# Where the spaced weight blocks lie against the streamed rows: one shift for 320 columns, one for 336

## The chip, the cores and the metric

The kernel runs on one core of a Trainium2 chip. The metric is the device time of one execution in microseconds (us), the median over several runs. TensorE (PE in the profile) multiplies: an instruction pair of a weight load (PEld) and a matmul, in which the loaded 128x128 weights stay and the columns of the other operand are streamed past them. ScalarE (ACT) and VectorE (DVE) prepare operands, GpSimd (POOL) does elementwise work beside them, and SyncE (SP) issues the transfers.

## The reference

One inference step of a hybrid decoder layer in float32, on 336 tokens (16 meta tokens, 256 of a prompt, 8 sequences of 8 new ones) of width 2048:

```python
h = rms_norm(x, norm_w)
proj = h @ w_in                       # 2048 x 20544
z, xbc, dt_raw, sc_b, sc_c, sc_h, sc_z, g_a, g_b = split_proj(proj)
# branch A: depthwise conv of width 4 on xbc, chunked state-space scan (SSD), gated group norm
y_a = y @ w_ssd_out                   # 4096 x 2048
# branch B: short conv of width 3
u_c = causal_dwconv(sc_c * sc_h, sconv_prev, sconv_w)
y_b = (sc_b * u_c * silu(sc_z)) @ w_sconv_out
merged = sigmoid(g_a) * y_a + sigmoid(g_b) * y_b
out = rms_norm(x + merged @ w_o, final_norm_w)
```

Beside it the new states of both convolutions and of the scan are returned.

## The kernel before, in words

Everything lies with channels on the 128 partitions and tokens along the row. A projection is cut into **units** of 128 output channels (`unit`, line 130). A unit takes the 2048 input channels in two halves; for each half `wblk` (line 96) brings one 128x1024 piece of weights (eight blocks of 128x128) and splits it in two: `hi`, rounded to the matmul's format by ACT (line 101), and `lo`, the rest, by DVE (line 102). The activations are kept split in the same way, in `hx` (halves `hhi` and `hlo`), for the first units in `uhi` and `ulo`, for the short convolution's output in `vhi` and `vlo`, for the scan's in `yh` and `yl`. A product is `hi*xh + hi*xl + lo*xh`, so a half has 3 x 8 = 24 matmuls (`mm`, line 125, all issued on line 127) and a unit 48, summed in one bank of the accumulator. Each matmul loads its own weights.

Three things say where the operands of a matmul lie and in which order they come.

The row of block `k` is `hhi[:, k, t0:T]`. Rows are 336 numbers (1344 bytes) apart, and `t0` is 0 (336 columns, for the scan's x and B), 12 (`TC`, 324 columns, for its C and for the inputs of the short convolution) or 16 (`META`, 320 columns, everything else). `vhi`, `vlo`, `yh` and `yl` have rows of 336 numbers too, of which 320 are used.

The weight blocks are **spaced** (`spaced`, line 93): a tile has room for 1280 numbers (`WB`), its blocks begin 144 numbers (`WS`, 576 bytes) apart, and the whole lies `16 * at` numbers, that is `at` times 64 bytes, behind the tile's start. `at` is given with each unit, from the names on line 91 or as `j % 4`.

The order of the 24 matmuls comes from `terms` (line 116) with one of three plans. RISE takes the eight rows upwards, first all `hi*xh`, then `hi*xl`, then `lo*xh`. TURNS takes `hi*xh` and `hi*xl` of a row one after the other. FALL2 takes the even rows downwards and then the odd ones, or the reverse, in steps of two.

The stages follow each other on PE in the order in which they are written. In the first (lines 183 to 340) the short convolution's inputs C and h (`conv_in`, lines 241 and 246), its gate z and its factor B (line 332) come for j = 0 to 15, the first of them on `uhi`. Then come 16 pairs of a gate unit g_b (line 448) and a unit of w_sconv_out on `vhi` (v, line 451). The third stage runs over eight groups of the scan: `weave` (line 789) interleaves units of the z (line 513), of the next group's B, C and x (`conv_tile`, line 471), of the output projection of the group before (`out_units`, line 747, four rows a product, 12 matmuls, on `yh`) and of the gate g_a (line 763) with the steps of the scan, which have their own small matmuls. Last come the remaining output and gate units and the projection w_o (line 853).

Nothing has costs or due times: the order on each engine is the order of the program. Weight tiles have three buffers each, so a transfer, a split and the matmuls of three successive halves overlap.

Of the kernel before, what the change touches and what calls it, by code (L numbers as in the profile page):

```python
# [9 lines left out]
AF = mybir.ActivationFunctionType  # L10
# [6 lines left out]
META = 16  # L17
TC = 12
TV = T - META
# [21 lines left out]
def fb(ap):  # L41
    return ap.bitcast(F32)
# [7 lines left out]
def tile_hybrid_step(ctx, tc, xT, w0, w1, w2, wdt, wso, wsc, wo, cmask, vec, hvec, convst, sconvst, xe_, fwe, h0T,  # L50
                     yA, yB, yE, convo, ssmp, ssms, sconvo):
    nc = tc.nc
    mult, add, sub = ALU.mult, ALU.add, ALU.subtract
# [33 lines left out]
    def col(base, i):  # L87
        return V[:, base + i:base + i + 1]

    latest = {}  # L90
    AT_S, AT_B, AT_G, AT_V, AT_Z, AT_H, AT_Y, AT_O = 3, 0, 1, 1, 2, 3, 1, 0

    def spaced(name, at):
        return wp.tile([P, WB], F32R, name=name)[:, 16 * at:16 * at + 8 * WS].rearrange("p (k m) -> p k m", m=WS)[:, :, :P]
# [16 lines left out]
                    tc.add_manual_dep(ins, a.name, mybir.DependencyInfo(mybir.DependencyClass.NoSync,  # L111
                                                                         mybir.DependencyReason.DATA), reason="step")

    RISE, TURNS, FALL2 = range(3)

    def terms(plan, hi, lo, xh, xl, nk):
        if plan == TURNS:
            return [(hi, x, k) for k in range(nk) for x in (xh, xl)] + [(lo, xh, k) for k in range(nk)]
        if plan == FALL2:
            even, odd = (list(range(i, nk, 2))[::-1] for i in range(2))  # L120
            return [(w, x, k) for w, x, q in ((hi, xh, even), (hi, xl, even), (hi, xl, odd), (hi, xh, odd), (lo, xh, odd),
                                              (lo, xh, even)) for k in q]
        return [(w, x, k) for w, x in ((hi, xh), (hi, xl), (lo, xh)) for k in range(nk)]

    def mm(out, hi, lo, xh, xl, base, nk, k0, first, last, plan=RISE):
        for i, (w, x, k) in enumerate(terms(plan, hi, lo, xh, xl, nk)):
# [3 lines left out]
    def unit(src, xh, xl, n, plan=RISE, at=0):  # L130
        pt = ps.tile([P, 512], F32, name="pj")
        for half in range(2):
            hi, lo = wblk(src[:, half * 1024:half * 1024 + 1024], at)
            mm(pt[:, :n], hi, lo, xh, xl, 0, 8, half * 8, half == 0, half == 1, plan)
        return pt[:, :n]

    def proj(src, t0, plan=RISE, at=0):
        return unit(src, lambda k: hhi[:, k, t0:T], lambda k: hlo[:, k, t0:T], T - t0, plan, at)
# [25 lines left out]
    def eights(ap, w=8):  # L164
        return ap.rearrange("p (b t) -> p b t", t=w)
# [17 lines left out]
    with tc.tile_pool(name="pa", bufs=2) as pa:  # L183
# [33 lines left out]
        for k in range(KT):  # L217
            split = nc.scalar.activation(uhi[:, k, :], ya[:, k, :], AF.Copy, scale=yan[:, k:k + 1])
            rest = nc.vector.scalar_tensor_tensor(ulo[:, k, :], ya[:, k, :], yan[:, k:k + 1], fb(uhi[:, k, :]), mult, sub)
            if k % 2 == 0:  # L220
                hi = wp.tile([P, WB], F32R, name="whi")
                lo = wp.tile([P, WB], F32R, name="wlo")
# [15 lines left out]
        def conv_in(j, pr, pre=None, fac=None, between=None):  # L238
            c_s = pa.tile([P, T - TC], F32, name="c_s")
            if fac is None:  # L240
                nc.scalar.activation(c_s, pre[0] if pre else pr(w2[16 + j], TC, FALL2, j % 4), AF.Copy)
            else:
                nc.vector.tensor_tensor(c_s, pr(w2[16 + j], TC, FALL2, j % 4), fac, mult)
            if between:
                between()
            ph = pre[1] if pre else pr(w2[32 + j], TC, TURNS, j % 4)
            up = pa.tile([P, 338], F32, name=f"up{j}" if j < 2 else "up", bufs=1 if j < 2 else 2)
            ups = eights(up[:, 258:338], 10)
            nc.vector.tensor_tensor(up[:, :258], c_s[:, 2:260], ph[:, 2:260], mult)  # L249
            nc.vector.tensor_tensor(ups[:, :, 2:10], eights(c_s[:, 260:]), eights(ph[:, 260:]), mult)  # L250
            return up, ups
# [71 lines left out]
        vhi = pa.tile([P, KT, T], F32R, name="vhi", bufs=1)[:, :, :TV]  # L323
        vlo = pa.tile([P, KT, T], F32R, name="vlo", bufs=1)[:, :, :TV]
        for j in range(KT):
            u = ((up0, ups0), (up1, ups1), u2)[j] if j < 3 else conv_in(j, proj)
            if j == 3:
                nc.sync.dma_start(HV, hvec)
                consts(C_SEG, C_ALL)
            if j < 2:  # L330
                continue
            rest = [(j, *u, lambda: proj(w2[48 + j], META, at=AT_S), lambda: proj(w2[j], META, at=AT_B))]
            if 4 < j < 7:
                o = j - 5
                rest.append((o, *((up0, ups0), (up1, ups1))[o], lambda: zf[o], lambda: bf[o]))
            for q, *a in rest:
                th = conv_out(q, *a)
                nc.scalar.activation(vhi[:, q, :], th, AF.Copy)
                nc.vector.tensor_tensor(vlo[:, q, :], th, fb(vhi[:, q, :]), sub)
# [105 lines left out]

        tab = tables(pa)
        for m in range(KT):
            pg = proj(w2[80 + m], META, at=AT_G)
            th = pa.tile([P, TV], F32, name="thg", tag="thz")
            nc.scalar.activation(th, pg, AF.Tanh, scale=0.5)  # L450
            py = unit(wsc[m], lambda k: vhi[:, k, :], lambda k: vlo[:, k, :], TV, at=AT_V)
            nc.vector.scalar_tensor_tensor(th, th, 1.0, py, add, mult)
            nc.sync.dma_start(mb_d[m], th)
            next(tab, None)
# [6 lines left out]
    with tc.tile_pool(name="pb", bufs=2) as pb:  # L461
# [7 lines left out]
        czs = CZ.rearrange("p (s i w) -> p s i w", s=2, w=40)  # L469

        def conv_tile(src, j, t0, out, cs):
            pp = proj(src, t0, TURNS if t0 else FALL2, j % 4)
            pad = pads[npad[0] % 2]
            npad[0] += 1
            smp = pad[:, 275:363].rearrange("p (b t) -> p b t", t=11)
            nc.scalar.activation(pad[:, 3 + t0:275], pp[:, :272 - t0], AF.Copy)  # L476
            nc.scalar.activation(smp[:, :, 3:11], pp[:, 272 - t0:].rearrange("p (b t) -> p b t", t=8), AF.Copy)
            nc.gpsimd.tensor_copy(smp[:, :, 0:3], cs[:, 1:9, :])  # L478
            nc.gpsimd.tensor_copy(cs[:, 0, :], pad[:, 272:275])  # L479
            nc.gpsimd.tensor_copy(cs[:, 1:9, :], smp[:, :, 8:11])  # L480
            i0 = META if t0 else 0
            acc = pb.tile([P, 360], F32, name="cacc")
            nc.scalar.activation(acc[:, i0:], pad[:, i0:360], AF.Identity, bias=col(V_CB, j), scale=col(V_CW, 4 * j))
            for k in range(1, 4):
                nc.vector.scalar_tensor_tensor(acc[:, i0:], pad[:, i0 + k:360 + k], col(V_CW, 4 * j + k),  # L485
                                               acc[:, i0:], mult, add)
            th = pb.tile([P, 360], F32, name="cth", bufs=1)
            nc.scalar.activation(th[:, i0:], acc[:, i0:], AF.Tanh)  # L488
            nc.vector.scalar_tensor_tensor(out[:, i0:272], th[:, i0:272], 1.0, acc[:, i0:272], add, mult)
            nc.vector.scalar_tensor_tensor(  # L490
                out[:, 272:].rearrange("p (b t) -> p b t", t=8),
                th[:, 272:360].rearrange("p (b t) -> p b t", t=11)[:, :, 3:11], 1.0,
                acc[:, 272:360].rearrange("p (b t) -> p b t", t=11)[:, :, 3:11], add, mult)
# [16 lines left out]
        def z_units(g, st):  # L510
            st["zs"] = []
            for t in range(4):
                pz = proj(w1[4 * g + t], META, at=AT_Z)
                z = pb.tile([P, TV + 4], F32, name="zs", bufs=4)
                th = pb.tile([P, 360], F32, name="cth", bufs=1)[:, :TV]
                nc.scalar.activation(th, pz, AF.Tanh, scale=0.5)
                nc.scalar.activation(z[:, :TV], pz, AF.Copy)
                nc.vector.scalar_tensor_tensor(z[:, :TV], th, 1.0, z[:, :TV], add, mult)
                st["zs"].append(z)
                yield  # L520
# [239 lines left out]

        def gate_units(m0, m1):
            for m in range(m0, m1):
                pg = proj(w2[64 + m], META, at=AT_H)
                if m < KT // 2:
                    th = pb.tile([P, 360], F32, name="cacc")[:, :TV]
                else:
                    th = pb.tile([P, TV + 4], F32, name="zs", bufs=4)[:, :TV]
                nc.scalar.activation(th, pg, AF.Tanh, scale=0.5)
                if m < KT // 2:
                    nc.sync.dma_start(sg_d[m], th)  # L770
                else:
                    old = pb.tile([P, 360], F32, name="cacc")[:, :TV]
                    nc.sync.dma_start(old, sg_d[m - KT // 2])
                    pair = [(q, t, fetch(q)) for q, t in ((m, th), (m - KT // 2, old))]
                    with tc.issue_after(latest["dve"]):
                        for q in pair:
                            merge(*q)
                yield
# [40 lines left out]
    with tc.tile_pool(name="pc", bufs=3) as pc_:  # L819
# [42 lines left out]
        for m in range(KE, KT):  # L862
# [3 lines left out]
            for half in range(2):  # L866
# [6 lines left out]
                for wide in ((True, False), (False, True))[half]:  # L873
                    for k in range(8):
                        w, x = (h, hx[:, :, 8 * half + k, :NA]) if wide else (l, hhi[:, 8 * half + k, :NA])
# [44 lines left out]
        fac = pc_.tile([P, NA], F32, name="fac", bufs=1)  # L920
# [129 lines left out]
```

## Time and profile before

| | |
|---|---|
| runs shown | 1812.24, 1812.73, 1813.86 us; median 1812.73 |
| the profiled execution | 1811.64 us, its span 1809.8 us |
| PE busy | 1802.9 us, 13006 matmul records |
| DVE, ACT, POOL busy | 1145.9, 830.4, 389.1 us |
| matmuls of line 127 | 11280 (7536 of 320 columns, 1824 of 324, 1920 of 336) |
| granted TensorE clock | 1.0 |

A matmul's busy time is the length of one instruction from its start to its modelled end, and successive ones overlap. How fast PE goes is read from the distance between starts in the order of time, not from that length.

### The profile page before, as it was taken

How to read it: one execution, taken by the hardware profiler on the slowest of the kernel's cores; microseconds unless marked ns; L12 is line 12 of the kernel's file. 1: busy time of each engine (PE TensorE's matmuls, PEld its weight loads, DVE VectorE, ACT ScalarE, POOL GpSimd, SP SyncE). 2: the span in 40 equal slices, each digit the busy share in tenths (PEclk: the TensorE clock that was granted, in tenths of full speed). 3: DMA queues.
4: the chain of work that ended last, by engine and by line, in shares of the span. 5: the costliest groups of instructions: out<-in, count | busy, mean ns of one | idle time of the engine just before them, and what ended most of it. 6: DMA issues, size and time to landing. Idle time of an engine off the chain costs nothing.

```text
span 1809.8 us, 32410 instructions
## 1 busy us (share of the span) xinstructions
PE 1802.9 (100%) x13006; PEld 1786.8 (99%) x13006; DVE 1145.9 (63%) x1696; ACT 830.4 (46%) x1269; POOL 389.1 (21%) x398
## 2 busy tenths in 40 slices
PE   9999999999999999999999999999999999999998
PEld 9999999999999999999999999999999999999998
DVE  7845544444543335668587777877878778776644
ACT  6433333333333334645656354564546546343543
POOL 0100000000000001153252433524334243400012
PEclk9999999999999999999999999999999999999999
DMA  7444444444544557457466574665746657476553
GB/s 257 146 152 148 151 151 148 149 152 154 155 158 163 164 164 233 147 180 248 151 205 226 176 244 152 209 216 180 244 153 216 205 169 253 154 244 213 185 178 130
DMA packets 117286, 331.33 MB, mean 183 GB/s; under 512 B 20944, under 2 KB 37904, under 8 KB 117136
## 3 DMA queue, kind: packets, MB, share of 16 engines
q1 hardware_dynamic: 116272, 327.89, 55.9%
q8 instruction: 102, 1.67, 0.4%
q10 hardware_dynamic: 864, 1.38, 0.2%
q14 instruction: 48, 0.39, 0.1%
HBM read 296.34 MB, written 32.88 MB: 182 GB/s over the span
## 4 chain that ended last, share of the span: by engine, by line
PE 99%; issue 0%; DVE 0%; POOLq 0%; POOL 0%; DVEq 0%
PE pj L127 92%; PE yb L664 2%; PE ms L650 1%; PE pj L232 1%; PE yb L599 1%; PE ms L548 1%; PE pj L876 1%; PE ms L232 0%; PE yb L727 0%; PE yb L902 0%; PE ms L551 0%; PE ms L201 0%; PE ms L550 0%; PE pj L352 0%; PE pj L351 0%; PE ms L712 0%
## 5 line engine op out<-in xcount | busy, mean ns | idle before, releaser
L127 PE MATMUL pj<-hx,whi 128*128 128x320 f32 (+2 forms) x5760 | 913.5, 310 | 0.0
L127 PEld LDWEIGHTS pj<-hx,whi 128*128 128x128 f32 x5760 | 863.9, 188 | 4.6 <-ACT pad L476 1.7
L102 DVE TENSOR_TENSOR wlo<-wraw,whi 128x1024 fp32r<-128x1024 f32 x470 | 595.3, 1267 | 403.9 <-PE pj L127 203.7
L101 ACT ACTIVATE whi<-wraw 128x1024 fp32r<-128x1024 f32 x470 | 497.2, 1058 | 751.7 <-PE pj L127 622.8
L127 PE MATMUL pj<-hx,wlo 128*128 128x320 f32 (+2 forms) x2880 | 483.2, 310 | 0.0
L127 PEld LDWEIGHTS pj<-hx,wlo 128*128 128x128 f32 x2880 | 439.6, 188 | 0.0
L610 POOL TENSOR_TENSOR h<-h,decS 128x512 f32<-128x512 f32 x64 | 76.4, 1228 | 147.5 <-PE ms L650 147.5
L255 POOL COPY SCS<-up 128x2 f32<-128x2 f32 x16 | 20.9, 1308 | 355.7 <-DVE up L249 325.5
L127 PE MATMUL pj<-yh,whi 128*128 128x320 f32 x512 | 96.7, 310 | 0.0
L127 PE MATMUL pj<-yl,whi 128*128 128x320 f32 x512 | 95.5, 308 | 0.0
L127 PE MATMUL pj<-yh,wlo 128*128 128x320 f32 x512 | 95.5, 308 | 0.0
L758 DVE TENSOR_TENSOR yan<-yan,pj 128x320 f32<-128x320 f32 x112 | 54.3, 485 | 63.0 <-PE pj L127 61.8
L485 DVE SCALAR_TENSOR_TENSOR cacc<-pad,V,cacc 128x360 f32<-128x360 f32 (+1 forms) x144 | 89.7, 623 | 2.0
L127 PEld LDWEIGHTS pj<-yh,whi 128*128 128x128 f32 x512 | 80.3, 188 | 2.0 <-issue 0.2
L478 POOL COPY pad<-cs 128x24 f32<-128x24 f32 x48 | 53.3, 1111 | 127.6 <-DVE cacc L485 115.9
L127 PEld LDWEIGHTS pj<-yl,whi 128*128 128x128 f32 x512 | 80.1, 187 | 0.0
L127 PEld LDWEIGHTS pj<-yh,wlo 128*128 128x128 f32 x512 | 80.1, 187 | 0.0
L479 POOL COPY cs<-pad 128x3 f32<-128x3 f32 x48 | 45.0, 938 | 80.6 <-ACT pad L476 80.1
L858 POOL TENSOR_TENSOR sacc<-sacc,sqf 128x320 f32<-128x320 f32 x13 | 15.4, 1181 | 191.5 <-ACT sqf L856 191.5
L582 POOL TENSOR_TENSOR xe<-xdt,tet 128x512 f32<-128x512 f32 (+1 forms) x24 | 30.3, 1264 | 105.6 <-DVE xdt L553 91.5
L488 ACT ACTIVATE cth<-cacc 128x360 f32<-128x360 f32 (+1 forms) x48 | 23.9, 498 | 39.9 <-DVE cacc L485 39.4
L127 PE MATMUL pj<-vhi,whi 128*128 128x320 f32 x256 | 42.0, 306 | 0.0
(284 smaller groups left out, 1646.0 us busy)
## 6 DMA issues: line engine op xcount, KB each, us to landing
wraw<-w SPq DMA_DIRECT2D x346, 512.0 KB, 3.8
wraw<-wso SPq DMA_DIRECT2D x64, 512.0 KB, 3.5
wraw<-wsc SPq DMA_DIRECT2D x32, 512.0 KB, 3.8
h<-h0T SPq DMA_DIRECT2D x32, 512.0 KB, 5.1
ssms<-h SPq DMA_DIRECT2D x32, 512.0 KB, 4.2
wraw<-wo SPq DMA_DIRECT2D x32, 512.0 KB, 3.8
xq_d<-xe SPq DMA_DIRECT2D x16, 320.0 KB, 3.4
W<-ac_d SPq DMA_DIRECT2D x8, 576.0 KB, 5.7
```

Of the source, the lines that this page charges most:

```text
L101: latest["act"] = nc.scalar.activation(hi, raw, AF.Copy).ins
L102: latest["dve"] = nc.vector.tensor_tensor(lo, raw, fb(hi), sub).ins
L127: latest["pe"] = nc.tensor.matmul(out, w[:, base + k], x(k0 + k), start=first and i == 0, stop=last and i == 3 * nk - 1).ins
L255: nc.gpsimd.tensor_copy(SCS[:, j, 0, :], up[:, 256:258])
L478: nc.gpsimd.tensor_copy(smp[:, :, 0:3], cs[:, 1:9, :])
L479: nc.gpsimd.tensor_copy(cs[:, 0, :], pad[:, 272:275])
L485: nc.vector.scalar_tensor_tensor(acc[:, i0:], pad[:, i0 + k:360 + k], col(V_CW, 4 * j + k), acc[:, i0:], mult, add)
L488: nc.scalar.activation(th[:, i0:], acc[:, i0:], AF.Tanh)
L582: nc.gpsimd.tensor_tensor(split(xe[c][:n]), split(xdt[c][:n]), bc(hv(tet[:n, c, :], g), [n, 8, HP]), mult)
L610: nc.gpsimd.tensor_tensor(split(h0[b]), split(h0[b]), bc(hv(decS[:, b, :], g), [P, 8, HP]), mult)
L664: nc.tensor.matmul(yb[q * HP:(q + 1) * HP, t, t0:t0 + n], x[:, h * HP:(h + 1) * HP], w[:, h, :], start=i == 0, stop=i == 3)
L758: nc.vector.tensor_tensor(ya[:, m, :TV], ya[:, m, :TV], pp[:, :TV], add)
```

## The change

The names of `at` become AT_V = 1, AT_Y = 3, AT_O = 3, AT_X = 1, AT_C = 2, AT_SC = 0; what has no name left takes `at` = 0. The plan TURNS is dropped. A plan LAST is added, which takes the rows upwards but begins with the last of the eight: 7, 0, 1, ... 6. The v units use it. `conv_tile` takes FALL2 for 324 columns as well as for 336. The h input of the short convolution goes from TURNS to RISE at the same `at` as before. With rows and blocks both 1 modulo 4 in units of 64 bytes, each unit's next weight block then begins, modulo 4, 1 unit past the row that is streamed where there are 320 columns (on `hx`, `vhi` and `yh`), and 0 units past it where there are 336. No instruction, transfer or wait is added or taken away.

```diff
-    AT_S, AT_B, AT_G, AT_V, AT_Z, AT_H, AT_Y, AT_O = 3, 0, 1, 1, 2, 3, 1, 0
+    AT_V, AT_Y, AT_O, AT_X, AT_C, AT_SC = 1, 3, 3, 1, 2, 0
...
-    RISE, TURNS, FALL2 = range(3)
+    RISE, LAST, FALL2 = range(3)
 
     def terms(plan, hi, lo, xh, xl, nk):
-        if plan == TURNS:
-            return [(hi, x, k) for k in range(nk) for x in (xh, xl)] + [(lo, xh, k) for k in range(nk)]
...
-        return [(w, x, k) for w, x in ((hi, xh), (hi, xl), (lo, xh)) for k in range(nk)]
+        return [(w, x, (k - (plan == LAST)) % nk) for w, x in ((hi, xh), (hi, xl), (lo, xh)) for k in range(nk)]
...
-                nc.scalar.activation(c_s, pre[0] if pre else pr(w2[16 + j], TC, FALL2, j % 4), AF.Copy)
+                nc.scalar.activation(c_s, pre[0] if pre else pr(w2[16 + j], TC, FALL2, AT_SC), AF.Copy)
...
-            ph = pre[1] if pre else pr(w2[32 + j], TC, TURNS, j % 4)
+            ph = pre[1] if pre else pr(w2[32 + j], TC, at=j % 4)
...
-            rest = [(j, *u, lambda: proj(w2[48 + j], META, at=AT_S), lambda: proj(w2[j], META, at=AT_B))]
+            rest = [(j, *u, lambda: proj(w2[48 + j], META), lambda: proj(w2[j], META))]
...
-            pg = proj(w2[80 + m], META, at=AT_G)
+            pg = proj(w2[80 + m], META)
...
-            py = unit(wsc[m], lambda k: vhi[:, k, :], lambda k: vlo[:, k, :], TV, at=AT_V)
+            py = unit(wsc[m], lambda k: vhi[:, k, :], lambda k: vlo[:, k, :], TV, LAST, AT_V)
...
-            pp = proj(src, t0, TURNS if t0 else FALL2, j % 4)
+            pp = proj(src, t0, FALL2, AT_C if t0 else AT_X)
...
-                pz = proj(w1[4 * g + t], META, at=AT_Z)
+                pz = proj(w1[4 * g + t], META)
...
-                pg = proj(w2[64 + m], META, at=AT_H)
+                pg = proj(w2[64 + m], META)
```

More of the change, by code (lines that the diff above doesn't have):

```diff
@@ L240, in conv_in @@
             if fac is None:
-                nc.scalar.activation(c_s, pre[0] if pre else pr(w2[16 + j], TC, FALL2, j % 4), AF.Copy)
+                nc.scalar.activation(c_s, pre[0] if pre else pr(w2[16 + j], TC, FALL2, AT_SC), AF.Copy)
             else:
-                nc.vector.tensor_tensor(c_s, pr(w2[16 + j], TC, FALL2, j % 4), fac, mult)
+                nc.vector.tensor_tensor(c_s, pr(w2[16 + j], TC, FALL2, AT_SC), fac, mult)
             if between:
                 between()
-            ph = pre[1] if pre else pr(w2[32 + j], TC, TURNS, j % 4)
+            ph = pre[1] if pre else pr(w2[32 + j], TC, at=j % 4)
             up = pa.tile([P, 338], F32, name=f"up{j}" if j < 2 else "up", bufs=1 if j < 2 else 2)
```

## The prediction

> **What bounds the kernel now.** I read the page's first lines, then the chain of waits, then the waits by engine, and last the order of time on TensorE.
>
> ```profile
> span 1809.8 us, 32410 instructions
> PE 1802.9 (100%) x13006; PEld 1786.8 (99%) x13006; DVE 1145.9 (63%) x1696; ACT 830.4 (46%) x1269; POOL 389.1 (21%) x398
> PEclk9999999999999999999999999999999999999999
> PE 99%; issue 0%; DVE 0%; POOLq 0%; POOL 0%; DVEq 0%
> L127 PE MATMUL pj<-hx,whi 128*128 128x320 f32 (+2 forms) x5760 | 913.5, 310 | 0.0
> L101 ACT ACTIVATE whi<-wraw 128x1024 fp32r<-128x1024 f32 x470 | 497.2, 1058 | 751.7 <-PE pj L127 622.8
> ```
>
> PE is busy for the whole span at the full granted clock, and 99% of the chain of waits is PE. The matmuls of L127 wait for nothing (idle before 0.0), and ACT, which splits the weights, waits 622.8 us for PE to give a weight buffer back. So the time is the number of matmuls times the distance from one start to the next. The 310 ns of a row is the length of one matmul, which overlaps its neighbours. The distance has to be read from the starts, in the order of time. In the fence below the columns are start, length of the merged piece, engine, line, operation and count. A unit of the projection is 48 matmuls (two halves of 24), so the start of a unit less that of the unit before, over 48, is the distance.
>
> ```profile
> 91.99 2.53 PE L127 MATMUL pj<-hx,whi 128*128 128x324 f32 x16
> 99.09 2.55 PE L127 MATMUL pj<-hx,whi 128*128 128x324 f32 x16
> 106.25 2.52 PE L127 MATMUL pj<-hx,whi 128*128 128x320 f32 x16
> 113.30 2.48 PE L127 MATMUL pj<-hx,whi 128*128 128x320 f32 x16
> 120.26 2.51 PE L127 MATMUL pj<-hx,whi 128*128 128x324 f32 x16
> 127.29 2.52 PE L127 MATMUL pj<-hx,whi 128*128 128x324 f32 x16
> ...
> 176.52 2.50 PE L127 MATMUL pj<-hx,whi 128*128 128x324 f32 x16
> 183.56 2.52 PE L127 MATMUL pj<-hx,whi 128*128 128x324 f32 x16
> 190.66 2.51 PE L127 MATMUL pj<-hx,whi 128*128 128x320 f32 x16
> 197.71 2.44 PE L127 MATMUL pj<-hx,whi 128*128 128x320 f32 x16
> 204.52 0.75 PE L127 MATMUL pj<-hx,whi 128*128 128x324 f32 x4
> ...
> 624.86 1.33 PE L127 MATMUL pj<-vhi,whi 128*128 128x320 f32 x8
> 626.02 1.30 PE L127 MATMUL pj<-vlo,whi 128*128 128x320 f32 x8
> 631.69 2.48 PE L127 MATMUL pj<-hx,whi 128*128 128x320 f32 x16
> 638.61 0.60 PE L127 MATMUL pj<-vhi,whi 128*128 128x320 f32 x3
> ```
>
> The reader is to see that the same instruction, 128x320, has several distances. Call **shift** the 64-byte unit in which the next weights begin, less the unit in which the row streamed now begins, modulo 4. The blocks of a spaced tile lie 9 units apart and the rows 21 (336 numbers), both 1 modulo 4; META (16 numbers) is 1 unit, TC (12) three quarters. The program of the kernel before puts the spaced tiles 1 unit past a multiple of 4, hx, yh and yl at 0, vhi, vlo and uhi at 2. So in rising order a unit with META has shift `at`+1, a wo unit `at`+2, an output unit (yh) `at`+2, a v unit `at`. The order FALL2 takes rows in steps of two: with all 336 columns its shift is `at`-1, with 324 it is `at`-1.75. Now the rows:
>
> - Shift 0, the z of the short convolution (S: 106.25 to 113.30, 7.05 us): 146.9 ns.
> - Shift 1, its B (113.30 to 120.26, 6.96 us): 145.0; but B from 197.71 to 204.52, 6.81 us: 141.9. So shift 1 has two steady patterns.
> - Shift 2, the gate g_b (G: 631.69 to 638.61, 6.92 us): 144.2.
> - Shift 1, v (624.86 to 631.69, 6.83 us): 142.3, made of 145.0 in its first 8 matmuls (to 626.02) and 5.67 us over 40 = 141.75 after them.
>
> **The change part by part.** It neither adds nor removes an instruction, a DMA or a wait. It writes the two halves of a weight tile at another offset (ACT 1058 ns, a DVE twin; same form, hidden under PE as the 622.8 us show) and reorders matmuls inside a unit. All that it can move is the distance. The other units touched:
>
> ```profile
> 701.15 2.62 PE L127 MATMUL pj<-hx,whi 128*128 128x336 f32 x16
> 708.52 2.57 PE L127 MATMUL pj<-hx,whi 128*128 128x336 f32 x16
> 715.74 2.61 PE L127 MATMUL pj<-hx,whi 128*128 128x336 f32 x16
> 723.01 2.65 PE L127 MATMUL pj<-hx,whi 128*128 128x336 f32 x16
> 730.48 0.75 PE L127 MATMUL pj<-hx,whi 128*128 128x320 f32 x4
> 737.52 2.51 PE L127 MATMUL pj<-hx,whi 128*128 128x320 f32 x16
> 741.04 0.45 PE L127 MATMUL pj<-hx,whi 128*128 128x320 f32 x2
> 1002.19 0.74 PE L127 MATMUL pj<-yh,whi 128*128 128x320 f32 x4
> 1003.95 0.45 PE L127 MATMUL pj<-yh,whi 128*128 128x320 f32 x2
> 1609.90 0.73 PE L127 MATMUL pj<-yh,whi 128*128 128x320 f32 x4
> 1611.60 0.59 PE L127 MATMUL pj<-yh,whi 128*128 128x320 f32 x3
> 1702.14 2.47 PE L127 MATMUL pj<-hx,whi 128*128 128x320 f32 x16
> 1709.05 0.45 PE L127 MATMUL pj<-hx,whi 128*128 128x320 f32 x2
> ```
>
> *320 columns, all to shift 1.* What distance will they have? The low end is 141.75 (v's steady part), the high end 145.0 (the first B). I take **142.4**: about four fifths of the matmuls in the first pattern and one fifth in the second, because v and one of the two B rows settle in the first, and since the units will mostly follow one another at the same shift, a pattern once reached has fewer occasions to be left. Matmuls are units times 48, 24 a weight tile for wso.
>
> - S, 14 units, 672: 146.9 to 142.4 is 4.5 ns, 3.0 us.
> - z of the SSD (Z, shift 3; 737.52 to 741.04 is 3.52 us over 24, 146.7), 32 units, 1536: 4.3 ns, 6.6 us.
> - g_a (H, shift 0 as S), 16 units, 768: 4.5 ns, 3.5 us.
> - output units in the weave (Y, shift 3; 1002.19 to 1003.95, 1.76 us over 12, 146.7), 56 tiles, 1344: 5.8 us.
> - G, 768: 144.2 to 142.4, 1.4 us. The wo units (O, shift 2; 1702.14 to 1709.05, 6.91 us, 144.0), 14 units, 672: 1.1 us.
> - B, 672, from the mean of its two rows, 143.5: 0.7 us.
> - v (768) and the last output units (1609.90 to 1611.60, 1.70 us over 12: 141.7; 192) stand at or under 142.4 already: together 0.2 us lost. Starting v from its last row makes the shift 1 at the borders from and to G too (in rising order they would be 2 and 0); it is worth at most the 8 x 3.25 ns of v's entry a unit, 16 units, 0.4 us, and lies in the 142.4.
>
> Sum 21.9 us over 7392 matmuls. Were all at 141.75 it would be 4.8 more, at 145.0 it would be 19.2 less.
>
> *336 columns, all to shift 0.* The four x units of the first group (701.15 to 730.48) have shifts 3, 0, 1, 2 and take 7.37, 7.22, 7.27 and 7.47 us: 153.5, 150.4, 151.5, 155.6. At the second's value they save 3.1, 0, 1.1 and 5.2 ns on 384 matmuls each: 3.6 us. The B units (8, 384 matmuls) run through the same four shifts twice: mean 152.75, 2.35 ns, 0.9 us. Ends: 150.4 is the lowest row; at the mean they would save nothing.
>
> *324 columns.* The first projection of the short convolution stands at `at` 3 (91.99 to 99.09, 147.9), 0 (120.26 to 127.29, 146.5) and 2 (176.52 to 183.56, 146.7); all go to 0: mean 147.0 to 146.5 on 624, 0.3 us. The C units of the SSD leave TURNS, which the h projection shows at 149.2 (99.09 to 106.25) and 147.9 (183.56 to 190.66), for FALL2 at the 146.7 of `at` 2: 1.9 ns on 384, 0.7 us. The h projection itself goes from TURNS to RISE at the same offsets; a whole unit of it in RISE is in no row. Its bounds are the highest and lowest 324 rows, 149.2 and 146.5 against a mean of 148.6: 0.4 us worse to 1.3 better on 624. I take 0.2 better, because a third of TURNS is in rising order already.
>
> All together 21.9 + 3.6 + 0.9 + 0.3 + 0.7 + 0.2 = **27.6 us**. The profiled execution took 1811.64 us (span 1809.8 and 1.84 around it), so 1784.0; the median of the runs shown is 1.09 higher, so **1785.1**.
>
> **What hides the rest.** If PE runs 1.5% faster, the splits must come 1.5% faster: per half a unit 1058 on ACT and, on DVE, the row below, against 3.42 us of matmuls (24 x 142.4). DVE's fullest slices are 8 tenths.
>
> ```profile
> DVE   7845544444543335668587777877878778776644
> L102 DVE TENSOR_TENSOR wlo<-wraw,whi 128x1024 fp32r<-128x1024 f32 x470 | 595.3, 1267 | 403.9 <-PE pj L127 203.7
> ```
>
> DVE too waits 203.7 us for PE at this line, so the cover holds. If it were gone in the eight groups of the SSD, their part of the sum (Z, Y, x, B, C and the gates in it, about 19 us) would be in question.
>
> The Trainium skill (TensorE: Matmul & The Clock Gate, "Step-by-step: what each phase is for") says that PE reads the streamed operand and the weights through two independent ports, so that loading the next weights takes no read bandwidth from the running matmul. By that rule the shift is worth nothing and the sum is 0. The rows of S and B, 146.9 against 141.9 for one form, speak against it.
>
> **The rivals.**
>
> 1. *The other pattern of shift 1.* 145.0 is as steady as 141.75. If after each break by the SSD's own matmuls, and after each 324 unit, the matmuls fall into it, the 320 columns gain 2.7 us instead of 21.9. For it: the first B. Against it: v. Time 1785.1 + 19.2 = 1804.3; with half of them so, 1794.7.
> 2. *Supply takes the place.* DVE becomes late in the groups and half of the 19 us goes: 1794.6. Against it: the 203.7 us.
> 3. *No effect.* The distance follows the neighbours in the stream and the place in the kernel, and the shift only goes along with them: each S comes after a 324 unit, each v after a G. Each unit keeps its distance: 1812.7. For it: shift 3 shows 146.7 in Y and 141.7 in the last output units. Against it: the x units, which differ in shift alone and run from 150.4 to 155.6.
> 4. *Slower.* The pattern is a lock between successive matmuls, kept from unit to unit; today the change of shift breaks bad ones, and with one shift everywhere the worst is kept: each width runs at its highest row. Then v loses 4.6 ns, G 2.7, O 2.9, B 3.4, the last output units 5.2 (3.5 + 2.1 + 1.9 + 2.3 + 1.0 = 10.8 us), and x and B units 155.6 less 152.75 on 1920, 5.5 us: 1829. The 320 columns average 145.4 now (142.4 plus 21.9 us / 7392); with the 5.7 us of the other units, 0.8 ns, it decides for slower from 146.2 on. Against it: v leaves 145.0 by itself within 8 matmuls and stays out:
>
> ```profile
> L127 PE MATMUL pj<-vlo,whi x256: 304/304/306, 465.9 to 685.4; 128*128 128x320 f32 x128
> ```
>
> All 256 matmuls of v's second pass have one length, in all 16 units.
>
> **How the numbers follow.** Forecast 0.76 (its own range 1779 to 1793: all 320 columns at 141.75 is 1780.3, four tenths more of them at 145.0 is 1793), rival 1 0.13 (1793 to 1805), rival 2 0.03, rival 3 0.04, rival 4 0.04. The range 1778 to 1800 holds the forecast, rival 2 and about half of rival 1. A measurement of this kernel can tell about 0.2%, 3.6 us, from no change: faster 0.92 (forecast, 1, 2), the same 0.04, slower 0.04.
>
> **What would show it.** Right: S, Z, H, Y, G and O units in the order of time at 6.80 to 6.85 us (1.70 for 12 matmuls of Y) with pieces 141.7 apart, x units all at 7.22, an unchanged number of instructions, PE still at 99% of the chain. Rival 1: B-like units of 6.96. Rival 2: a PE wait for `wlo` L102 that isn't there now. Wrong: S or Z units still at 7.05, or x units that still differ among themselves; then the shift isn't what sets the distance.

## The result, and the profile after

| | runs shown | median us | ratio to before, 95% interval |
|---|---|---|---|
| before | 4 (1812.24 to 1813.86) | 1812.95 | |
| changed | 4 (1786.97 to 1791.06) | 1789.39 | 0.9869 [0.9852, 0.9886] |

The change makes the kernel 23.6 us faster; 27.6 were forecast. The profiled execution of the changed kernel took 1786.97 us, which is its fastest run, 24.7 us below the profiled one of before. All lines after the dropped plan have moved up by two: line 127 is now 125, 621 is 619.

First the page of the changed kernel: span, engines, chain of waits and two groups.

```profile
span 1785.2 us, 32410 instructions
PE 1776.8 (100%) x13006; PEld 1760.2 (99%) x13006; DVE 1147.4 (64%) x1696; ACT 829.1 (46%) x1269; POOL 392.7 (22%) x398
PE 90%; DVE 4%; DMA 3%; ACT 2%; issue 1%; POOLq 0%; SPq 0%; POOL 0%; ACTq 0%; DVEq 0%
L102 DVE TENSOR_TENSOR wlo<-wraw,whi 128x1024 fp32r<-128x1024 f32 x470 | 599.5, 1276 | 389.2 <-PE pj L125 193.2
L125 PE MATMUL pj<-yh,whi 128*128 128x320 f32 x512 | 95.0, 307 | 1.5 <-ACT zs L515 0.8
```

The instructions are the same in number, and ACT and DVE have the same work to do. What is new is the third line: PE is 90% of the chain of waits, not 99%, and DMA, DVE and ACT have come into it. The last line shows where: the output units wait 0.8 us for ACT, which reads the scan's z out of the accumulator (`zs`, line 515); before, no matmul of that line did.

The units themselves, from the order of time on PE (start, length, engine, line, operation, count), in the places that the prediction quoted of before:

```profile
105.67 2.48 PE L125 MATMUL pj<-hx,whi 128*128 128x320 f32 x16
...
112.63 2.48 PE L125 MATMUL pj<-hx,whi 128*128 128x320 f32 x16
...
119.59 2.55 PE L125 MATMUL pj<-hx,whi 128*128 128x324 f32 x16
...
613.99 2.43 PE L125 MATMUL pj<-hx,whi 128*128 128x320 f32 x16
620.78 1.29 PE L125 MATMUL pj<-vhi,whi 128*128 128x320 f32 x8
627.59 2.43 PE L125 MATMUL pj<-hx,whi 128*128 128x320 f32 x16
...
696.23 2.58 PE L125 MATMUL pj<-hx,whi 128*128 128x336 f32 x16
703.45 2.57 PE L125 MATMUL pj<-hx,whi 128*128 128x336 f32 x16
710.67 2.57 PE L125 MATMUL pj<-hx,whi 128*128 128x336 f32 x16
717.88 2.57 PE L125 MATMUL pj<-hx,whi 128*128 128x336 f32 x16
725.09 2.43 PE L125 MATMUL pj<-hx,whi 128*128 128x320 f32 x16
...
1692.35 2.43 PE L125 MATMUL pj<-hx,whi 128*128 128x320 f32 x16
1699.15 0.45 PE L125 MATMUL pj<-hx,whi 128*128 128x320 f32 x2
```

A gate and a v unit take 6.79 and 6.81 us, a wo unit 6.80: over 48 that is 141.5 to 141.9 ns. All four x units take 7.21 or 7.22 us, where before they ran from 7.22 to 7.47. But S and B at 105.67 and 112.63 take 6.96 us each, 145.0 ns. Both patterns of shift 1 are there, side by side.

To see where the gain lies, I added up the distance from each matmul's start to the next one's over the whole trace, by kind of unit. Column "gain" is before less after:

| kind | before us | after us | gain | predicted |
|---|---|---|---|---|
| S, z of the short convolution | 98.58 | 96.54 | 2.04 | 3.0 |
| Z, z of the SSD | 227.44 | 221.89 | 5.55 | 6.6 |
| H, g_a | 112.93 | 109.54 | 3.39 | 3.5 |
| Y, output units in the weave | 198.72 | 193.93 | 4.79 | 5.8 |
| G, g_b | 110.94 | 109.31 | 1.63 | 1.4 |
| O, wo units | 96.70 | 95.21 | 1.49 | 1.1 |
| B of the short convolution | 96.42 | 96.32 | 0.10 | 0.7 |
| v and the last output units | 136.98 | 136.64 | 0.34 | -0.2 |
| x, 336 columns | 236.46 | 232.50 | 3.96 | 3.6 |
| B of the SSD, 336 columns | 59.49 | 58.47 | 1.02 | 0.9 |
| C of the SSD, 324 columns | 57.20 | 56.08 | 1.12 | 0.7 |
| C and h of the short convolution | 184.73 | 184.34 | 0.39 | 0.5 |
| the SSD's own matmuls | 136.67 | 138.03 | -1.36 | 0 |

The 320 columns gave 19.3 us of the forecast 21.9, the other widths 6.5 of 5.7, and the scan's own matmuls lost 1.4. A distance holds whatever PE waited in it, so the new waits lie in Y and in the last line; there, 1.3 of the 1.4 us lie in the scan matmuls of line 549, behind which waiting output units come.

### The profile page after: what moved, and what is told of

Read it like the earlier page. It is cut to its first block, busy times and chain, and to the rows that moved or that the text cites. A ratio compares the mean times of both kernels' runs of the same rounds, so it can differ in the third digit from the quotient of the medians.

```text
span 1785.2 us, 32410 instructions
## 1 busy us (share of the span) xinstructions
PE 1776.8 (100%) x13006; PEld 1760.2 (99%) x13006; DVE 1147.4 (64%) x1696; ACT 829.1 (46%) x1269; POOL 392.7 (22%) x398
## 4 chain that ended last, share of the span: by engine, by line
PE 90%; DVE 4%; DMA 3%; ACT 2%; issue 1%; POOLq 0%; SPq 0%; POOL 0%; ACTq 0%; DVEq 0%
PE pj L125 83%; DMA wraw<-w 2%; PE yb L662 2%; DVE wlo L102 1%; DMA ssms<-h 1%; PE ms L648 1%; PE pj L230 1%; DVE h L728 1%; DVE cacc L483 1%; ACT whi L101 1%; PE yb L597 1%; ACT W L571 1%; PE pj L874 1%; PE ms L230 0%; PE ms L546 0%
## 5 line engine op out<-in xcount | busy, mean ns | idle before, releaser
L125 PE MATMUL pj<-hx,whi 128*128 128x320 f32 (+2 forms) x5760 | 899.9, 308 | 0.0
L125 PEld LDWEIGHTS pj<-hx,whi 128*128 128x128 f32 x5760 | 851.6, 188 | 4.6 <-ACT pad L474 1.7
L102 DVE TENSOR_TENSOR wlo<-wraw,whi 128x1024 fp32r<-128x1024 f32 x470 | 599.5, 1276 | 389.2 <-PE pj L125 193.2
L125 PE MATMUL pj<-hx,wlo 128*128 128x320 f32 (+2 forms) x2880 | 476.3, 307 | 0.0
L125 PEld LDWEIGHTS pj<-hx,wlo 128*128 128x128 f32 x2880 | 433.2, 188 | 0.0
L125 PE MATMUL pj<-vhi,wlo 128*128 128x320 f32 x256 | 41.5, 304 | 0.0
```

What stands on the lines that cost most here:

```text
L102: latest["dve"] = nc.vector.tensor_tensor(lo, raw, fb(hi), sub).ins
L125: latest["pe"] = nc.tensor.matmul(out, w[:, base + k], x(k0 + k), start=first and i == 0, stop=last and i == 3 * nk - 1).ins
```

## The experiments

No kernel here leaves out or changes any part of the computation. Each time is the median of its runs; "before" is the kernel before, run beside it on the same chip. Edits are against the changed kernel.

### All 320 columns at another shift

Theory: the shift sets the distance. Rivals: it only goes along with the place and the neighbours (rival 3), or with the history on PE. One number per kind puts all 7392 matmuls with 320 columns at shift 0, 2 or 3; the plans, the order of units and all else stay.

```diff
-    AT_V, AT_Y, AT_O, AT_X, AT_C, AT_SC = 1, 3, 3, 1, 2, 0
+    AT_V, AT_Y, AT_O, AT_X, AT_C, AT_SC, AT_M = 0, 2, 2, 1, 2, 0, 3   # shift 0
+    AT_V, AT_Y, AT_O, AT_X, AT_C, AT_SC, AT_M = 2, 0, 0, 1, 2, 0, 1   # shift 2
+    AT_V, AT_Y, AT_O, AT_X, AT_C, AT_SC, AT_M = 3, 1, 1, 1, 2, 0, 2   # shift 3
...
-    def proj(src, t0, plan=RISE, at=0):
+    def proj(src, t0, plan=RISE, at=AT_M):
```

> The changed kernel with all units of 320 columns on hx, vhi and yh at shift 0 instead of 1 (the 336 and 324 columns as changed). My theory, the shift alone sets the distance: S stood at shift 0 before at 146.7 ns, so all 7392 matmuls of 320 columns go there, about 4.1 ns more than now, 30 us: 1817 to 1820 us. Theory that the shift has no effect (the place in the kernel sets the distance): as the changed kernel, 1789 us. Theory that history decides: something between, with units of 320 columns at several distances.

> The same with shift 2 for all units of 320 columns. My theory: G and O stood at shift 2 before at 144.0 ns, so 1.4 ns more than now on 7392 matmuls, 10 us: 1798 to 1801 us. No effect of the shift: 1789 us.

> The same with shift 3 for all units of 320 columns. Before, Z and Y stood at shift 3 at 146.7 ns and the last output units at 141.7, so shift 3 has two patterns. My theory with the slow one everywhere: 1817 to 1820 us. If a pattern that is reached is kept from unit to unit while the shift stays the same (history), long chains (the g_b and v units, the last output, gate and w_o units) may stand at 141.7 and the time is 1800 to 1812 us. No effect: 1789 us.

| shift of the 320 columns | median us | before us | ratio |
|---|---|---|---|
| 0 | 1816.25 | 1813.18 | 1.0016 [1.0006, 1.0025] |
| 1 (the change) | 1789.39 | 1812.95 | 0.9869 [0.9852, 0.9886] |
| 2 | 1798.00 | 1813.18 | 0.9916 [0.9901, 0.9931] |
| 3 | 1816.62 | 1813.18 | 1.0018 [1.0009, 1.0027] |

One gate unit and the v unit after it, in the order of time on PE, with shift 0, then 2, then 3:

```profile
665.09 2.51 PE L125 MATMUL pj<-hx,whi 128*128 128x320 f32 x16
...
672.13 1.33 PE L125 MATMUL pj<-vhi,whi 128*128 128x320 f32 x8
```

```profile
657.86 2.47 PE L125 MATMUL pj<-hx,whi 128*128 128x320 f32 x16
...
664.76 1.32 PE L125 MATMUL pj<-vhi,whi 128*128 128x320 f32 x8
```

```profile
666.98 2.51 PE L125 MATMUL pj<-hx,whi 128*128 128x320 f32 x16
...
674.02 1.34 PE L125 MATMUL pj<-vhi,whi 128*128 128x320 f32 x8
```

The gate unit takes 7.04, 6.90 and 7.04 us, so 146.7, 143.8 and 146.7 ns, against 6.79 in the changed kernel. Rival 3 falls: the same units in the same places change their distance with the shift alone, and the kernel as a whole with them. At each shift the kinds stand at three different offsets `at` (v; Y and O; the rest) and yet run at nearly the same distance: at shift 2 G at 144.3, v at 144.0, O at 143.9 ns, each the mean over its units. So it is the place of the weights against the row that counts, not their offset alone. The times at shift 0 and 3 lie just under what the first expectation gave (1817 to 1820 us).

For shift 3 the second expectation, that long chains of equal units settle at the 141.7 which the last output units showed before, failed as a time: the long chains stay at 146.7. But four whole units of shift 3 do run at 141.7, the first two Z units (the first at 738.23, 6.80 us) and the first two gate units of the last group, each time until matmuls of the scan come in between:

```profile
738.23 2.43 PE L125 MATMUL pj<-hx,whi 128*128 128x320 f32 x16
...
745.03 2.43 PE L125 MATMUL pj<-hx,whi 128*128 128x320 f32 x16
```

So shift 3 has two steady patterns, as shift 1 has. The shift says which distances there are, and not by itself which of them a unit gets.

### The x units back to four shifts

```diff
-            pp = proj(src, t0, FALL2, AT_C if t0 else AT_X)
+            pp = proj(src, t0, FALL2, AT_C if t0 else j % 4)
```

> The changed kernel with the units of 336 columns at shifts 3, 0, 1, 2 again, as before the change; nothing else undone. My theory: the 4.9 us that the trace of the changed kernel shows for x and B units go back: 1794 us. No effect: 1789 us.

Measured 1793.72 us, 0.9892 [0.9877, 0.9907] to a before of 1813.18. The first x units of the third stage in the order of time:

```profile
696.40 2.63 PE L125 MATMUL pj<-hx,whi 128*128 128x336 f32 x16
...
703.79 2.57 PE L125 MATMUL pj<-hx,whi 128*128 128x336 f32 x16
...
711.00 2.61 PE L125 MATMUL pj<-hx,whi 128*128 128x336 f32 x16
...
718.28 2.65 PE L125 MATMUL pj<-hx,whi 128*128 128x336 f32 x16
725.75 2.47 PE L125 MATMUL pj<-hx,whi 128*128 128x320 f32 x16
```

They take 7.39, 7.21, 7.28 and 7.47 us again, the four values of before to 0.02. The sum of the x units goes from 232.50 to 236.64 us, that of the SSD's B from 58.47 to 59.55. So by the trace 5.2 us of the change's gain come from here, where the prediction had 3.6 + 0.9; the median is 4.3 us above the changed kernel's. The Z units, in which nothing was changed, lose 1.3 us beside it (221.89 to 223.17): 17 of them are slow instead of nine. So what another kind of unit does moves them between their two patterns.

### What chooses between the two patterns of shift 1

In the changed kernel 7 of the 14 pairs of S and B have 145.0, and they are the pairs whose h unit before them (324 columns, `j % 4`) stands at offset 2 or 3 on `hx`; the first pair, behind an h unit at offset 2 on `uhi`, is fast. Theory: the pattern is chosen when a unit begins, by what runs before it, and kept. Then an h input that always stands at offset 0 makes all S and B fast. Rival: it is chance, or the place in the kernel, and half the pairs stay slow. The kernel called ph0 puts it at offset 0; it ran beside the changed kernel itself (after_again).

```diff
-            ph = pre[1] if pre else pr(w2[32 + j], TC, at=j % 4)
+            ph = pre[1] if pre else pr(w2[32 + j], TC, at=0)
```

> The changed kernel itself, to stand beside the next three on the same chip: 1787 to 1791 us, as measured.

> The changed kernel with the h input of the short convolution at offset 0 for every j instead of j modulo 4. In the trace of the changed kernel the z and B units after it run at 141.7 ns where its offset is 0 or 1, and at 145.0 where it is 2 or 3. Theory: which of the two patterns of shift 1 a run of units takes is set by how the unit ahead of it ends, so with offset 0 all 14 pairs of z and B are fast: 7 pairs x 96 x 3.3 ns = 2.2 us less, the units of C after them 0.5 us and the first gate and v pair 0.3 us less, 3.0 us together: 1784 to 1788, ratio to the changed kernel about 0.998. Rival, that the pattern goes with j or with the place: no change.

Measured 1788.93 us for the changed kernel (0.9862 [0.9846, 0.9879] to 1813.63) and 1785.81 with h at offset 0 (0.9848 [0.9833, 0.9862]). The unit that stands at 105.67 above, in the second kernel:

```profile
105.59 2.45 PE L125 MATMUL pj<-hx,whi 128*128 128x320 f32 x16
...
112.42 2.43 PE L125 MATMUL pj<-hx,whi 128*128 128x320 f32 x16
...
119.22 2.50 PE L125 MATMUL pj<-hx,whi 128*128 128x324 f32 x16
```

S takes 6.83 us here and B 6.80, where the same two had 6.96. No pair is slow, nor any G or v unit. The sums: S 96.54 to 95.53, B 96.32 to 95.20, the C input 0.47 less, G and v 0.30 less: 2.9 us of an expected 3.0. Neither S nor B was touched: the unit ahead of them decides. The medians differ by 3.1 us, but the runs overlap (1788.29 to 1790.20 against 1783.99 to 1788.82), so it is the trace that shows this one.

The same test from the other side: the plan TURNS is put back for the h input and for the C units of the SSD, with `j % 4`.

```diff
-            ph = pre[1] if pre else pr(w2[32 + j], TC, at=j % 4)
+            ph = pre[1] if pre else pr(w2[32 + j], TC, TURNS, j % 4)
...
-            pp = proj(src, t0, FALL2, AT_C if t0 else AT_X)
+            pp = proj(src, t0, TURNS if t0 else FALL2, j % 4 if t0 else AT_X)
```

> The changed kernel with the plan TURNS at offsets j modulo 4 again for the h input of the short convolution and for the scan's C. By the traces of before and after the C units lose 1.1 us and the h input 0.2 us; the z and B units behind the h input enter shift 1 from another order and may settle otherwise, 2 us in either direction: 1788 to 1792, the C units at 6.95 to 7.05 us instead of 6.87.

Measured 1790.39 us, 0.9865 [0.9847, 0.9884]. The C units lose 1.1 us (56.08 to 57.21), the h input 0.15, but S and B gain 1.3, because with TURNS ahead of them only 3 pairs are slow, now those behind an h unit at offset 0. Two parts of the change thus work against each other: its new plan for h is a little better in itself and sends more of the units behind it into the slow pattern. The time as a whole can't be told from that of the changed kernel.

### v from its last row

```diff
-            py = unit(wsc[m], lambda k: vhi[:, k, :], lambda k: vlo[:, k, :], TV, LAST, AT_V)
+            py = unit(wsc[m], lambda k: vhi[:, k, :], lambda k: vlo[:, k, :], TV, RISE, AT_V)
```

> The changed kernel with v in rising order again instead of from its last row: the shift stays 1 inside v and g_b units, but is 2 at the border from g_b to v and 0 at the border from v to g_b. Theory of the borders (a break of the shift makes the matmuls settle anew): v pays its entry again as before the change, 0.4 us in all, and the g_b units may settle in the slow pattern, up to 16 x 48 x 3.3 ns = 2.5 us: 1789.5 to 1792. Rival, that a border costs nothing: 1789.

Measured 1789.67 us, 0.9872 [0.9855, 0.9888], the time of the changed kernel. In the trace v loses 0.36 us and G 0.28 (one G unit goes to 145). The prediction gave at most 0.4 for v. As a time it can't be told from nothing.

### Where PE's new waits come from

PE's waits and the SP queue's wait at the state loads, in the second profile of the changed kernel, from the waits by engine (what waited, what for, total us, times, longest):

```profile
PE pj L125 <- ACT zs L515: 2.0, 1, 2.0
PE pj L125 <- DVE yan L756: 0.3, 1, 0.3
...
SPq L619 <- DMA ssms<-h: 36.5, 28, 2.9
```

The chain of waits in the same profile (start, length, what):

```profile
1496.64 5.54 DMA ssms<-h
...
1502.67 7.57 DMA wraw<-w
...
1520.82 1.04 ACT whi L101
...
1522.18 0.33 ACT zs L515
...
1522.56 3.56 PE pj L125 x12
```

and the SP queue at that place:

```profile
1498.28 0.34 SPq L98 DMA_DIRECT2D wraw<-w  x1
1500.99 1.57 SPq L619 DMA_DIRECT2D h<-h0T  x2
1502.67 0.37 SPq L98 DMA_DIRECT2D wraw<-w  x1
```

By these starts SP takes its transfers one after the other. Two loads of the scan's initial states stand between two weight transfers; they need a buffer whose contents are still being written out (`ssms`, 5.54 us), so the next weight transfer starts 4.39 us after the last one. ACT comes to its splits late (`whi`; two pieces of the scan's own work on ACT, 2.55 and 2.03 us of line 571, lie in the same chain), the reading of z out of the accumulator (`zs`) stands behind them on ACT, and the output unit on PE waits for that. Theory: PE now comes early enough for this queue to set its pace in each group, and moving these loads to a place where the write-out is over takes the waits away. Rival: the supply as a whole is too slow, and the waits only move. The loads are moved from behind `rows(1)` to behind `decay(1)` ("..." stands for the loop's body).

```diff
             rows(1)
-            for u in range(4): ... nc.sync.dma_start(h, h0T[g, :, 2 * u:2 * u + 2, :]) ...
             yield
             weights(0)
             yield
             halve(0)
             decay(1)
+            for u in range(4): ... nc.sync.dma_start(h, h0T[g, :, 2 * u:2 * u + 2, :]) ...
             yield
```

> The changed kernel with the four loads of the scan's states moved two steps later in each group. Theory: the few us that the median of the changed kernel lies above the sum are PE waiting late in a group's beginning, because these loads wait on SP's queue for the states of the group before to be written (SP waits 38.1 us for that, 28 times), and the weight transfers stand behind them. Moved back, they find the writes done: SP's wait at the state load goes below 5 us, PE's gaps over 265 ns beside the fixed ones go (1.8 us in the profiled execution), and the time falls by 2 to 4 us, to 1785 to 1787. Rival, that DVE and ACT are simply full there: the gaps stay, no change.

> Both edits: if both theories hold the gains add, 5 to 7 us less than the changed kernel, 1782 to 1784. If only the first holds 1786, if neither 1789.

Measured 1784.61 us (runs 1784.55 to 1785.61; 0.9841 [0.9826, 0.9855]) for the move alone, all runs under all runs of the changed kernel, and 1782.28 (0.9826 [0.9811, 0.9841]) with the h input at offset 0 as well: the two gains nearly add (3.1 and 4.3 us alone, 6.7 together). PE's waits in the move alone, and the SP queue there:

```profile
PE pj L839 <- POOL rs_r L835: 0.3, 1, 0.3
...
SPq L624 <- DMA ssms<-h: 26.8, 21, 2.4
```

```profile
1495.97 0.34 SPq L98 DMA_DIRECT2D wraw<-w  x1
1498.09 0.34 SPq L624 DMA_DIRECT2D h<-h0T  x1
1499.53 0.33 SPq L98 DMA_DIRECT2D wraw<-w  x1
```

Both of PE's new waits are gone. But half of the theory failed: SP was to wait less than 5 us at the state loads, and it still waits 26.8 us, 21 times. What changed is what stands in between. One load is now between two weight transfers where there were two, and the weights start after 3.56 us instead of 4.39. If SP's wait itself cost time, moving the loads further back should gain again; the next kernel moves them behind `decay(2)`, with h at offset 0.

```diff
             decay(1)
-            for u in range(4): ... nc.sync.dma_start(h, h0T[g, :, 2 * u:2 * u + 2, :]) ...
             yield
...
             decay(2)
+            for u in range(4): ... nc.sync.dma_start(h, h0T[g, :, 2 * u:2 * u + 2, :]) ...
             yield
```

> The kernel with both edits of the second set, with the loads of the states moved four steps further back. In the trace of the first move SP still waits for the written states at these loads (26.8 and 31.3 us), though PE's gaps are gone. Theory: what counts is only which transfers stand behind the wait, and none that PE needs soon does any more: the wait changes, the time stays, 1781.5 to 1783. Rival: the wait still costs, and the time falls by another 1 to 2 us.

Measured 1781.59 us (1781.48 to 1782.46; 0.9825 [0.9810, 0.9841]) against 1782.28 (1781.52 to 1782.52): no difference that can be told, with SP still waiting 27.0 us, 21 times (one wait of PE for `zs`, 0.2 us, is back). SP's wait as such costs nothing that can be told; what stands behind it on the queue does. Whether the second load or the earlier place did the harm, these two moves don't separate.

That PE waits because it has become faster is not shown. The kernels at shift 0 and 3 are slower than before, and in each of them PE waits 0.5 us for `zs` too; at shift 0 the chain of waits through this place has a write-out of 7.19 us in it (`ssms`, at 1074.83):

```profile
1099.67 0.86 PE L125 MATMUL pj<-yh,whi 128*128 128x320 f32 x4 [0.47 <-ACT zs L515]
```

And in the kernel before the same two loads stand between two weight transfers, once for 4.97 us (1072.53 to 1077.50), and PE does not wait. So moving the loads is shown to take the waits away; how long a hold the kernel bears, and why the profile of before has none, stays open.

### Z from its last row

With both mended, the slow Z units were left: 3 of 4 in the third, fifth and seventh group. If a unit's first matmul decides, another first matmul in Z, nothing else changed, can move them. To the kernel with h at offset 0 and the loads behind `decay(1)`:

```diff
-                pz = proj(w1[4 * g + t], META)
+                pz = proj(w1[4 * g + t], META, LAST)
```

> The kernel with both edits of the second set, with the z units of the scan beginning with their last row (as v does); shift 1 inside. In groups 2, 4 and 6 three of four z units stand at 145.0, in the other groups none. Theory, the entry after a break decides which of the two patterns holds: the set of slow z units changes with nothing but the order of rows, so the time moves by something between -1.4 us (all fast) and +3.3 us (all slow). Rival, that the group or its buffers decide: groups 2, 4, 6 stay slow, no change, 1782.3.

Measured 1780.82 us, 0.9820 [0.9805, 0.9835], the lowest median of all: 32.2 us under before, 8.6 under the change. Against the kernel without this edit (1782.28, measured on another chip) the intervals overlap, so again the trace decides. The first half of the second Z unit of the third group, without and with it:

```profile
946.54 2.48 PE L125 MATMUL pj<-hx,whi 128*128 128x320 f32 x16
...
950.02 2.48 PE L125 MATMUL pj<-hx,whi 128*128 128x320 f32 x16
```

```profile
946.29 2.43 PE L125 MATMUL pj<-hx,whi 128*128 128x320 f32 x16
...
949.69 2.43 PE L125 MATMUL pj<-hx,whi 128*128 128x320 f32 x16
```

It goes from 3.48 to 3.40 us, 145.0 to 141.7 ns. All Z units are fast, 221.89 to 220.51 us in sum.

## Why the prediction was right, point by point

**What bounds the kernel: right.** The time was the number of matmuls times their distance, and the distance came down.

**The shift sets the distance: shown.** Four kernels that differ in it alone take 1789, 1798, 1816 and 1817 us. Rival 3 is against these numbers: the same unit takes 6.79, 6.90 or 7.04 us by where the next weights lie. The rule of the Trainium skill (TensorE: Matmul & The Clock Gate, "Step-by-step: what each phase is for"), by which the streamed operand and the weights have independent read ports and loading the next weights takes no read bandwidth from the running matmul, does not account for them. Why the place of the next weights matters, no run here shows. Nor is the shift everything: at shift 1 and at shift 3 whole units run at either of two distances.

**The size of "I take 142.4": mis-sized.** The figure itself was near (19.3 us of 21.9), but not how it came about. The mixture isn't a fraction spread over all units. H, O, G, v and most of Z are at 141.7 but for a few units; S and B are slow in half of their pairs, whole units long, and Z in nine units. That is why S gave 2.0 of 3.0 and B 0.1 of 0.7 (seven B units were slow before, seven are now), while O and G gave more than forecast. The reason given, that a pattern once reached has fewer occasions to be left, holds for both patterns: S and B stay slow for 96 matmuls. The inference from v, that 145.0 is left within 8 matmuls, does not carry over to units on `hx`. For S and B the unit ahead decides: with h at offset 0 2.9 us more are gained, which is all that was missing here. So a part of rivals 1 and 4 was true.

**x and B of the SSD, C: right, a little small.** "At the second's value" came out for every x unit (7.21 or 7.22), 5.0 us measured for 4.5; C gave 1.1 for 0.7. Undoing each gives it back (5.2 and 1.1).

**v from its last row: right.** At most 0.4 us, in the noise of a time.

**The cover holds: wrong.** This is the step that failed: "DVE too waits 203.7 us for PE at this line, so the cover holds". It still waits 193.2 us, and yet PE waits. A sum of slack over the whole kernel doesn't show the single places where the splits come late, here behind loads that hold the weights back for 4.4 us on the SP queue. "PE still at 99% of the chain" came out as 90% and 95% in two profiles. Rival 2 was thus true in kind, but by the queue and not by DVE's work, and in size about 4 us (1788.93 to 1784.61) instead of 9.5. The row that pointed to the place was in the waits of before: there the SP queue waited 32.9 us, 28 times, for the same write-out, without PE waiting for it. By its size it was no warning, since 26.8 us of it remain where PE no longer waits.

```profile
SPq L621 <- DMA ssms<-h: 32.9, 28, 2.8
```

The sum, then: all distances of the projection gave 25.8 us of the forecast 27.6 (19.3 and 6.5), and PE's waits took back 1.4 in the scan's own matmuls of the profiled run. That run is the fastest of the four; the median lies 2.4 us above it. The second profile, of a slower run, has the longer waits, and with the loads moved all runs lie within 1.1 us, so I put the spread of 1787 to 1791 down to these waits as well; it was not traced run by run, and the kernel before spreads by 2.7 us over 19 runs without such a wait in its profile.

## What to carry to other kernels

Where one engine is the bound at full clock, read the distance between starts for each kind of work, not its busy time: here equal instructions differed by 3% by how their operands lay. Where there are two steady patterns under equal conditions, look at what runs ahead: here the unit before the slow one was the one to mend. Before taking a supply as covered, look at what stands behind the waits of the transfer queue, place by place, and try a move; the sum of its waits said nothing here, neither before the loads were moved nor after.

## What had not been expected of the hardware

**A pattern with memory.** 128x320 matmuls at shift 1 run at 141.7 or 145.0 ns for whole units, and a different matmul ahead of them changes which one. Shift 3 has 146.7 and, in four whole units, 141.7. Shift 0 too has more than one: 146.7 in the gate units, 148.3 in the wo units (3.56 us over 24, from 1715.70 to 1719.26 in the kernel with shift 0).

**A short pause halves the clock.** In the second profile of the changed kernel PE waits 1.98 us, and then twelve matmuls take 3.36 us, 280 ns each. PE in the order of time, and two stretches (length; busy time and count of PE, PEld, DVE, ACT, POOL; granted clock; DMA share; GB/s):

```profile
1522.56 1.44 PE L125 MATMUL pj<-yh,whi 128*128 128x320 f32 x4 [1.98 <-ACT zs L515]
...
1525.92 0.89 PE L597 MATMUL yb<-xw,bh 128*128 128x512 f32 x3
```

```profile
1520.20:1522.50 2.30, 0.38 (x3) 0.12 (x1) 1.46 (x2) 2.30 (x5) 0.00 (x0) 1.00 0.10 9
1522.50:1525.40 2.90, 2.84 (x11) 2.85 (x12) 2.23 (x6) 0.47 (x3) 1.04 (x1) 0.51 0.74 243
```

The granted clock falls to 0.51 right after the pause and costs about 12 x 138 ns = 1.7 us more, nearly as much as the pause. The Trainium skill (TensorE: Matmul & The Clock Gate, "HAM oscillation — how this bites in real kernels") warns of pauses of more than about 3.4 us; here one of 2 us sufficed. In the kernel with TURNS a wait of 1.86 us did it too (granted clock 0.55 over the 3.2 us from 1523.3). One of 1.77 us in the kernel with v in rising order did not (1.00 over the 3.2 us from 1522.2), nor one of 1.26 us with the x units spread, nor those of 0.8 us at most in the other profile of the changed kernel. These are single cases, and they don't show what decides between 1.77 and 1.86.
